# Two transformer blocks on one core: first tiles reordered behind nine warming products, bias sign on ScalarE, gate logs in steps, modulation sums three stages later, squares in one tile

## The chip, the cores and the metric

The kernel runs on one core of one Trainium2 chip. The metric is the device time of one execution in microseconds (us). Engines: PE is TensorE (PEld its weight loads), DVE is VectorE, ACT is ScalarE, POOL is GpSimd, SP issues most DMAs. Each engine works through its own instructions in program order and waits where an operand is not ready.

## The reference, cut to what matters

```python
h = concat(meta_tokens, x)                       # 16 + 512 rows of 1024
u = rms_norm(h, norm_mix); proj = u @ w_in       # q, k, v, forget logits, conv, gates
o_a = windowed attention with sinks (bias table) # 8 heads, blocks of 128
log_f = log_sigmoid(fl + fox_forget_bias)        # 8 heads x 528
o_f = attention with cumsum(log_f); o_c = gated linear recurrence
h = h + (sum of gated branches) @ w_out
h = h + (silu(u2 @ gate) * (u2 @ up)) @ w_ffn_out
x = rms_norm(h, norm_final)                      # end of block one
mod = c @ w_ada + b_ada                          # 6 x 1024, needed by block two only
z = rmsnorm(x) * (1 + scale1) + shift1           # block two: mLSTM, differential
...                                              # attention, 32 experts, top 2
```

All of it is fp32.

## The kernel before, in words

Every dense product is made from three fp32r products: operands are split into a rounded high part (ACT copies) and a remainder (DVE subtracts), and high x high, high x low and low x high are summed in one PSUM bank. A *unit* is 128 output columns: 24 products of 512 columns for a depth of 1024. `pairA` runs two units interleaved over the depth, `unitA` one. Activations are stored with features on the partitions and 528 token columns.

**Weights.** `Stream` loads tiles of 1 MB in a fixed order (`order`) through SP into three slots; `split` makes the two parts of one unit (ACT copy L492, DVE subtract L493) into three pairs of part buffers; `ahead` splits whatever finds a free pair, `fill` issues a load for every free slot. SP issues in order, and a load waits at the head of the queue until the slot's last reader is done. The modulation tiles (`ada`, 24 chunks) stand in the same order; chunk n is summed on DVE (`ada_chunk`, two instructions of 1024 elements, L561) in `after()` behind the plan entry that `ada_at` names: the 4 `wo` entries take chunks 0 to 3, the first FFN-in entries chunks 4, 5, 6 and so on.

**Interleaving by hand.** A unit calls `tick()` after its depth steps 1, 3 and 5 and at its end. `later` holds generators that each advance one step per tick, `bg` a queue of attention pipes. So a generator's `yield` says after how many products its next instructions stand in each engine's order.

**The head.** `st.first` loads the first weight tile in two halves and splits them; `v_prep` makes the high part of input tile k (L753) and its square (L755) on ACT; `v_fin` the low part (L758) and the running sum of squares (L761) on DVE. Behind `pairA` stand `sum_rows` (column sums by products with a column of ones, L698, over the two tiles `acc` and `sqs[7]`), the row scale by `rsqrt` on 5 columns, one unit, `spread` (L692), the copies to `rb` on ACT (L774, L775) and `qa_out` on DVE (L779). `u_tiles` then makes the eight normed tiles (ut L789, uh L790 on ACT, ul L793) one per tick. The bias table `nbias` (1 MB) is loaded by SP (L799) and its sign turned on POOL (L800). The units for ka and va follow; `to_natural` copies va on ACT (L814) and transposes it on PE (L818) one tick later; then the units on the normed tiles begin.

**The forget gate.** After the unit `fl`, `log_sigmoid` (Abs, Exp, Ln on ACT; L717 to L719), a subtract, a memset and a scan run on DVE (L720, L917, L918) without a tick between; the result goes to DRAM and comes back broadcast (`load_cum`, POOL queue). The attention pipe `swa` shares ACT and DVE with it: scores minus bias L849, exponent L854, scale L860, transposes on PE L870.

**The first FFN units.** f = 0, 1, 2 run on un-normed input; their outputs are scaled afterwards in `normed` (L1204 to L1208, then the split L686, L687). `f_tiles` makes the normed input for f = 3 on: nt on DVE (L1193), fh on ACT (L1194), fl on POOL (L1197), one tile per tick.

**The end of block one.** `ff_last` runs the last FFN-out units in two token halves; squares on ACT (L1273, L1276) are added on POOL (L1277) into a first tile, and tile 7 keeps its own, so that `sum_rows` reads two tiles. `z_half` then makes the row scales (L1375 to L679), spreads them on PE (L692) and makes the z tiles (L1386, L1387, L1389). `Z1` and `Z2` say how many steps of it are taken at each product group of the next stage. The shared constants' slice `LATE` holds the vector c until the last modulation sum, and is loaded with constants afterwards.

Of the kernel before, what the change touches and what calls it, by code (L numbers as in the profile page):

```python
# [20 lines left out]
D = 1024  # L21
# [22 lines left out]
Z2 = ((1, 1, 1, 1, 1, 0, 0, 0), (0, 0, 1, 0, 0, 2, 2, 2))  # L44
# [314 lines left out]
def tile_kernel(ctx: ExitStack, tc: tile.TileContext, ws, ada, c_d, hT_d, cst_d, seq_d, bd_d, wr_d, pos_d, out):  # L359
# [54 lines left out]
    class Stream:  # L414
# [32 lines left out]
        def first(self):  # L447

            t = self.slots.popleft()
            self.raw[self.order[0]] = t  # L450
            self.lp = 1
            hs = [(j, slice(512 * i, 512 * i + 512)) for i in range(2) for j in range(2)]
            v = t.rearrange("p (j c) -> p j c", j=2)
            d = ws[0].rearrange("p (j c) -> p j c", j=2)
            for _, c in hs[::2]:
                nc.sync.dma_start(v[:, :, c], d[:, :, c])
                yield
            parts = []
            for j in range(2):
                self.done[j] = self.used[j] = self.parts.popleft()  # L460
                parts.append(self.done[j])
            self.sp = 2
            for n, (j, c) in enumerate(hs):
                if n == 2:
                    yield
                h, l = parts[j]
                S.copy(h[:, c], v[:, j, c])
                V.tensor_sub(l[:, c], v[:, j, c], h[:, c].bitcast(FT))
            self.free(self.order[0])
# [66 lines left out]
    ada_at = {n_wo + n: n for n in range(n_ada)}  # L536
# [179 lines left out]
    def log_sigmoid(out_t, x, tmp):  # L716
        S.activation(tmp, x, AF.Abs)  # L717
        S.activation(tmp, tmp, AF.Exp, scale=-1.0)
        S.activation(tmp, tmp, AF.Ln, bias=1.0)  # L719
        V.scalar_tensor_tensor(out_t, x, 0.0, tmp, op0=OP.min, op1=OP.subtract)  # L720

# [14 lines left out]

    halves = st.first()
    for k in range(0, 8, 2):
        nc.sync.dma_start(hT[k // 4][:, k % 4:k % 4 + 2], hT_d[:, k:k + 2])
        if k < 6:  # L740
            next(halves)
# [4 lines left out]
    acc = SM([128, T], name="acc")  # L746
    sqs = {}

    def v_prep(k):
        if k == 3:  # L750
            for _ in halves:
                pass
        S.mul(X(vh, k), X(hT, k), C("nm", k, k + 1))  # L753
        sqs[k] = acc if k == 0 else SM([128, T], name="sq")
        S.activation(sqs[k], X(hT, k), AF.Square)  # L755

    def v_fin(k):
        V.scalar_tensor_tensor(X(vl, k), X(hT, k), C("nm", k, k + 1), X(vh, k).bitcast(FT), op0=OP.mult,  # L758
                               op1=OP.subtract)
        if 0 < k < 7:  # L760
            V.tensor_add(acc, acc, sqs[k])  # L761

    set_ring([0, 1, 2, 3])
    first = pairA(v_h, v_l, v_prep, v_fin, XS)
    sum_rows(bank[4], 0, [acc, sqs[7]], 4, NM)
    sum_rows(bank[4], 4, [acc, sqs[7]], 1, 0)
    r5 = [ST([128, 16], name=f"r5{i}") for i in range(4)]
    V.tensor_scalar(r5[0][:, :5], bank[4][:, :5], 1.0 / D, EPS, op0=OP.mult, op1=OP.add)
    rsqrt(r5[1][:, :5], r5[0][:, :5], (r5[2][:, :5], r5[3][:, :5]))
    first += unitA(v_h, v_l, one_bank)  # L770
    spread(r5[1], bank[5])
    PE.matmul(bank[6][:, :NM], lhsT=r5[1][:, 4:5].to_broadcast([128, 128]), rhs=ident[:, :NM], start=True, stop=True)
    rb = SM([128, T], name="rb")
    S.copy(rb[:, NM:], bank[5])  # L774
    S.copy(rb[:, :NM], bank[6][:, :NM])  # L775
# [5 lines left out]
    for t in range(3):  # L781
        qa_out(t, first[t])
    ut = {}
# [12 lines left out]
    ug = later.add(u_tiles())  # L796
    qa_out(3, unitA(v_h, v_l, one_bank)[0])
    nbias = B([128, 8, 256], name="nbias")
    nc.sync.dma_start(nbias, seq_d)  # L799
    G.tensor_scalar(nbias, nbias, -1.0, None, op0=OP.mult)  # L800
# [29 lines left out]
    later.finish(ug)  # L830
# [79 lines left out]
    p = uT()  # L910
    lf = SM([8, T], name="lf")
    l2 = SM([8, T], name="l2")
    cum = SM([8, T], name="cum")
    for h in range(2):
        V.tensor_scalar(cum[:, HALF[h]], p[h][:8], C("fbias")[:8], None, op0=OP.add)
    log_sigmoid(lf, cum, l2)
    V.memset(l2, 1.0)  # L917
    V.tensor_tensor_scan(cum, l2, lf, 0.0, op0=OP.mult, op1=OP.add)  # L918
    cum_d = dpool.tile([8, T], FT, name="cum_d")
    G.dma_start(cum_d, cum)  # L920
# [8 lines left out]
    load_cum(0)  # L929
# [281 lines left out]
    def ff_in(gi):  # L1211
        a0, b0 = FGROUPS[gi]
        ah, al = [], []
        for f in range(a0, b0):
# [4 lines left out]
            if f < 3:  # L1219
# [17 lines left out]
                continue  # L1237
            w = SM([128, 512], name="fw")
# [18 lines left out]
    def ff_last(gi, steps):  # L1257
# [5 lines left out]
        def part(t, cs):  # L1263
            wh, wl = us[t][1:]
            p = DB()
            mm3([(p[:, cs], cs)], lambda i: wh[:, i], lambda i: wl[:, i], ah, al, nk, mid=False)
            h = X(hx, t)[:, cs]
            V.tensor_add(h, h, p[:, cs])
            for parts, scale in ((sums, 1.0), (sums_n, C("nfin", t, t + 1))):
                if t in (0, 7):  # L1270
                    if t == 0 or cs is TOK[0]:
                        parts.append(SM([128, 512], name="sq"))
                    S.activation(parts[-1][:, cs], h, AF.Square, scale=scale)  # L1273
                else:
                    sq = SM([128, 512], name="sq")
                    S.activation(sq[:, cs], h, AF.Square, scale=scale)  # L1276
                    G.tensor_add(parts[0][:, cs], parts[0][:, cs], sq[:, cs])  # L1277
# [20 lines left out]
    G.dma_start(cst[:, LATE], cst_d[:, LATE])  # L1298
# [1053 lines left out]
```

## Time and profile before

| what | before |
|---|---|
| median of 3 runs (lowest, highest) | 1619.85 us (1619.43, 1620.01) |
| the profiled execution, its own time | 1618.47 us |
| its span from first to last instruction | 1616.7 us |
| PE busy in the span | 1537.2 us (95%) |
| DVE, ACT, POOL busy | 923.3, 657.0, 201.2 us |
| mean granted TensorE clock | 0.987 of full |
| DMA | 258.28 MB, mean 160 GB/s |

The span is cut into windows; a window tells how long each engine was busy in it, how many instructions that were, and the clock granted to PE. The list of waits says whose result an engine stood for. The timeline gives start, duration and idle time before each instruction. In the last fifth of the span the DMA engines are busy nine tenths or more of the time; before it they are not.

### The profile page before, as it was taken

The page shows a single profiled execution, that of the slowest core. Times are in us where ns is not written, and L with a number is a line of the kernel's source. Part 1 is how long each engine was busy: PE and PEld are TensorE (multiplying, and loading weights), DVE is VectorE, ACT ScalarE, POOL GpSimd, SP SyncE. Part 2 cuts the span into 40 slices and gives each one's busy share as a digit, 9 for nine tenths or more (in the row PEclk, how much of TensorE's full clock was granted, in tenths as well). Part 3 has the DMA queues.
Part 4 walks back from the last instruction along what each step waited for, and adds up shares of the span by engine and source line. Part 5 has one row for each costly group of instructions (what it writes and reads, how often), then busy time and mean ns, then how long its engine had stood idle before and what let it go on. Part 6 is the DMA issues. An engine that isn't in the chain of part 4 may idle for free. (4 is left out here: it accounts for less than half of the span.)

```text
span 1616.7 us, 22593 instructions
## 1 busy us (share of the span) xinstructions
PE 1537.2 (95%) x8524; PEld 1153.4 (71%) x8524; DVE 923.3 (57%) x2020; ACT 657.0 (41%) x1208; POOL 201.2 (12%) x255
## 2 busy tenths in 40 slices
PE   7899999999999899999999999999999999998883
PEld 6788777788888778888889887778888874433321
DVE  5655455455757676664444755873466445565443
ACT  4445443326534332222233545653233215665442
POOL 0100111020030200000002142200013102111101
PEclk9999999999999999999999999999999999999997
DMA  5221221222235255445222241222223866999992
GB/s 187 92 79 67 92 80 53 79 91 79 103 137 215 104 209 208 181 186 193 105 83 100 79 143 54 78 79 85 95 82 134 312 234 258 388 404 392 395 390 65
DMA packets 49327, 258.28 MB, mean 160 GB/s; under 512 B 7316, under 2 KB 15636, under 8 KB 21184
## 3 DMA queue, kind: packets, MB, share of 16 engines
q1 hardware_dynamic: 41680, 237.17, 38.6%
q0 software_dynamic: 7248, 19.65, 4.2%
q8 instruction: 67, 1.10, 0.3%
q14 instruction: 44, 0.36, 0.1%
q10 hardware_dynamic: 288, 0.01, 0.0%
HBM read 250.48 MB, written 14.71 MB: 164 GB/s over the span
## 5 line engine op out<-in xcount | busy, mean ns | idle before, releaser
L493 DVE TENSOR_TENSOR wp<-wr,wp 128x1024 fp32r<-128x1024 f32 (+1 forms) x198 | 246.1, 1246 | 198.5 <-ACT wp L492 197.8
L492 ACT CAST wp<-wr 128x1024 fp32r<-128x1024 f32 (+1 forms) x198 | 204.2, 1035 | 111.3 <-PE bank L601 82.2
L599 PE MATMUL bank<-uh,wp 128*128 128x512 f32 (+1 forms) x464 | 150.7, 361 | 5.5 <-DVE ka L806 4.5
L601 PE MATMUL bank<-ul,wp 128*128 128x512 f32 (+1 forms) x464 | 144.4, 348 | 0.0
L603 PE MATMUL bank<-uh,wp 128*128 128x512 f32 (+1 forms) x464 | 144.1, 347 | 0.0
L599 PE MATMUL bank<-fh,wp 128*128 128x512 f32 x304 | 119.3, 392 | 6.6 <-ACT wp L492 6.6
L603 PE MATMUL bank<-fh,wp 128*128 128x512 f32 x304 | 119.2, 392 | 0.6 <-DVE wp L493 0.5
L601 PE MATMUL bank<-fl,wp 128*128 128x512 f32 x304 | 119.1, 392 | 0.4 <-POOL fl L1197 0.4
L599 PE MATMUL bank<-z,wp 128*128 128x512 f32 x264 | 108.4, 411 | 0.0
L603 PE MATMUL bank<-z,wp 128*128 128x512 f32 x264 | 103.3, 391 | 0.0
L601 PE MATMUL bank<-z,wp 128*128 128x512 f32 x264 | 102.9, 390 | 0.0
L599 PEld LDWEIGHTS bank<-uh,wp 128*128 128x128 f32 x464 | 81.0, 190 | 24.1 <-issue 6.8
L603 PEld LDWEIGHTS bank<-uh,wp 128*128 128x128 f32 x464 | 81.1, 190 | 11.2
L601 PEld LDWEIGHTS bank<-ul,wp 128*128 128x128 f32 x464 | 81.0, 190 | 9.8
L2197 ACT COPY wd<-wb 128x512 f32 x108 | 60.7, 616 | 55.9 <-DMA wb<-in_ws_dram 21.1
L2204 PE MATMUL bank<-wd,xT 128*32 128x512 f32 x512 | 78.5, 603 | 0.9 <-DVE wd L2197 0.6
L599 PE MATMUL bank<-ah,wp 128*128 128x512 f32 (+1 forms) x218 | 76.1, 349 | 0.0
L601 PE MATMUL bank<-al,wp 128*128 128x512 f32 (+1 forms) x218 | 75.9, 348 | 0.0
L603 PE MATMUL bank<-ah,wp 128*128 128x512 f32 (+1 forms) x218 | 75.9, 348 | 0.0
L599 PEld LDWEIGHTS bank<-fh,wp 128*128 128x128 f32 x304 | 57.6, 189 | 19.2 <-ACT wp L492 7.4
L603 PEld LDWEIGHTS bank<-fh,wp 128*128 128x128 f32 x304 | 57.4, 189 | 13.6 <-DVE wp L493 1.7
L601 PEld LDWEIGHTS bank<-fl,wp 128*128 128x128 f32 x304 | 57.5, 189 | 12.8 <-POOL fl L1197 0.8
(627 smaller groups left out, 3186.5 us busy)
## 6 DMA issues: line engine op xcount, KB each, us to landing
wr<-in_ws_dram SPq DMA_DIRECT2D x115, 1024.0 KB, 4.8
wb<-in_ws_dram SPq DMA_DIRECT2D x54, 1024.0 KB, 20.3
wr<-in_ada_dram SPq DMA_DIRECT2D x24, 1024.0 KB, 5.2
wq<-in_ws_dram SPq DMA_DIRECT2D x21, 1024.0 KB, 24.0
wr<-in_ws_dram SPq DMA_DIRECT2D x4, 768.0 KB, 4.2
ncb<-cum_d POOLq DMA_DIRECT2D x8, 264.0 KB, 3.7
wr<-in_ws_dram SPq DMA_DIRECT2D x4, 512.0 KB, 5.3
h_d<-row SPq DMA_DIRECT2D x8, 256.0 KB, 4.1
```

The lines of the kernel that those rows point to most:

```text
L492: S.copy(h[:, :fl], t)
L493: eng.tensor_sub(l[:, :fl], t, h[:, :fl].bitcast(FT))
L599: PE.matmul(ps, lhsT=wh(k), rhs=rh(k, sl), start=first and k == 0, stop=False)
L601: PE.matmul(ps, lhsT=wh(k), rhs=rl(k, sl), start=False, stop=False)
L603: PE.matmul(ps, lhsT=wl(k), rhs=rh(k, sl), start=False, stop=last and k == nk - 1)
L2197: (V.tensor_copy if j < 2 else S.copy)(t[:, j], w[:, bass.ds(regs[q][j], 512)])
L2204: PE.matmul(ps[c], lhsT=x(c), rhs=w(j), start=first, stop=last)
```

## The change

Nine products of 256 columns (identity times a zeroed tile, fp32) are issued before anything else on PE. The first half of the first weight tile is loaded as two transfers of 256 columns, ahead of input tiles 2 and 3. The high and low parts of input tiles 0 and 1 come first, then the weight splits, then tiles 2 and 3; squares come after the last input tile and are all summed into `hsq[0]` on DVE. Row sums, row scale, spread, rb and the first three `qa_out` become a generator, `norm_1`, stepped inside the next two units; `sum_rows` reads one tile instead of two. The bias load is issued before those units, and its sign is turned by two ACT multiplications of 1024 columns in `norm_1`. The gate's logarithm becomes a generator with Abs and Exp, Ln, subtract, scan one or two ticks apart, and its memset goes to POOL. Modulation chunks 4 to 23 move three plan entries later, and the reload of `LATE` with them to f = 19. In `ff_last` tile 7's squares are added on POOL as well, `sum_rows` reads one tile, and the second half's sums are one product group later.

```diff
-Z2 = ((1, 1, 1, 1, 1, 0, 0, 0), (0, 0, 1, 0, 0, 2, 2, 2))
+Z2 = ((1, 1, 1, 1, 1, 0, 0, 0), (0, 0, 0, 1, 0, 2, 2, 2))
...
-            for _, c in hs[::2]:
-                nc.sync.dma_start(v[:, :, c], d[:, :, c])
+            for cs in ((slice(0, 256), slice(256, 512)), (slice(512, 1024),)):
+                for c in cs:
+                    nc.sync.dma_start(v[:, :, c], d[:, :, c])
                 yield
...
-    ada_at = {n_wo + n: n for n in range(n_ada)}
+    ada_at = {n_wo + n + (3 if n > 3 else 0): n for n in range(n_ada)}
...
+            PE.matmul(bank[7][:, :256], lhsT=ident, rhs=mbig[:, :256], start=True, stop=True)
+    warm_up(9)
...
+    def v_mul(k):
+        S.mul(X(vh, k), X(hT, k), C("nm", k, k + 1))
+        V.scalar_tensor_tensor(X(vl, k), X(hT, k), C("nm", k, k + 1), X(vh, k).bitcast(FT), op0=OP.mult,
+                               op1=OP.subtract)
+    def h_square(k):
+        hsq[k] = SM([128, T], name="sq")
+        S.activation(hsq[k], X(hT, k), AF.Square)
+        if k:
+            V.tensor_add(hsq[0], hsq[0], hsq[k])
     def v_prep(k):
-        if k == 3:
+        if k == 2:
+            v_mul(2)
+            v_mul(3)
             for _ in halves:
                 pass
...
+        elif k > 3:
+            v_mul(k)
     def v_fin(k):
...
+        if k == 6:
+            for n in (1, 2):
+                h_square(n)
+    for k in range(2):
+        v_mul(k)
+    h_square(0)
+    next(halves)
     first = pairA(v_h, v_l, v_prep, v_fin, XS)
...
+    for k in range(3, 8):
+        h_square(k)
+    def norm_1():
+        yield
+        yield
+        sum_rows(bank[4], 0, hsq[:1], 4, NM)
+        sum_rows(bank[4], 4, hsq[:1], 1, 0)
+        V.tensor_scalar(r5[0][:, :5], bank[4][:, :5], 1.0 / D, EPS, op0=OP.mult, op1=OP.add)
+        rsqrt(r5[1][:, :5], r5[0][:, :5], (r5[2][:, :5], r5[3][:, :5]))
+        for t in range(4):
+            yield
+            if t % 2 == 0:
+                S.mul(nbias[:, 2 * t:2 * t + 4], nbias[:, 2 * t:2 * t + 4], -1.0)
+        spread(r5[1], bank[5])
...
+        S.copy(rb[:, NM:], bank[5])
+        S.copy(rb[:, :NM], bank[6][:, :NM])
+        for t in range(2):
+            qa_out(t, first[t])
+        yield
+        qa_out(2, first[2])
+        ug.append(later.add(u_tiles()))
...
     nc.sync.dma_start(nbias, seq_d)
-    G.tensor_scalar(nbias, nbias, -1.0, None, op0=OP.mult)
+    later.add(norm_1())
+    first += unitA(v_h, v_l, one_bank)
+    qa_out(3, unitA(v_h, v_l, one_bank)[0])
...
+    def forget_sums(p):
...
+        S.activation(l2, cum, AF.Abs)
+        S.activation(l2, l2, AF.Exp, scale=-1.0)
+        yield
+        S.activation(l2, l2, AF.Ln, bias=1.0)
+        yield
+        yield
+        V.scalar_tensor_tensor(lf, cum, 0.0, l2, op0=OP.min, op1=OP.subtract)
+        G.memset(l2, 1.0)
+        yield
+        V.tensor_tensor_scan(cum, l2, lf, 0.0, op0=OP.mult, op1=OP.add)
+        G.dma_start(cum_d, cum)
+        load_cum(0)
+    later.add(forget_sums(uT()))
...
+            if f == 19:
+                G.dma_start(cst[:, LATE], cst_d[:, LATE])
...
-                if t in (0, 7):
-                    if t == 0 or cs is TOK[0]:
-                        parts.append(SM([128, 512], name="sq"))
-                    S.activation(parts[-1][:, cs], h, AF.Square, scale=scale)
+                if t == 0:
+                    parts.append(SM([128, 512], name="sq"))
+                    S.activation(parts[0][:, cs], h, AF.Square, scale=scale)
                 else:
...
     ff_out(0)
-    G.dma_start(cst[:, LATE], cst_d[:, LATE])
```

## Rows read from the trace of the kernel before

**Rows 1.** Windows: length; busy us (count) of PE, PEld, DVE, ACT, POOL; clock; DMA

```profile
8.80:15.00 6.20, 6.12 (x14) 4.45 (x15) 5.04 (x9) 6.20 (x12) 0.00 (x0) 1.00 1.04 420
...
23.18:25.33 2.15, 2.15 (x22) 2.15 (x20) 0.00 (x0) 1.28 (x2) 0.00 (x0) 1.00 0.00 0
25.33:29.00 3.67, 3.67 (x11) 2.90 (x11) 3.12 (x14) 0.00 (x0) 0.00 (x0) 0.54 0.02 4
...
51.10:55.62 4.52, 0.00 (x1) 0.03 (x1) 4.52 (x9) 2.33 (x4) 1.30 (x1) 1.00 0.00 0
55.62:60.00 4.38, 4.38 (x16) 3.20 (x17) 4.03 (x8) 2.01 (x4) 0.00 (x0) 0.61 0.37 97
...
138.20:140.34 2.14, 0.40 (x4) 0.18 (x2) 2.07 (x9) 0.02 (x1) 0.53 (x1) 1.00 0.05 8
140.34:145.90 5.56, 5.56 (x33) 4.54 (x33) 2.89 (x10) 3.02 (x10) 2.05 (x4) 0.69 0.44 118
...
519.60:530.40 10.80, 10.80 (x49) 8.97 (x48) 6.16 (x11) 2.76 (x4) 0.00 (x0) 1.00 0.52 200
...
554.96:560.49 5.53, 0.15 (x1) 0.00 (x0) 3.76 (x8) 2.19 (x3) 1.49 (x1) 0.77 0.53 190
560.49:564.84 4.35, 4.31 (x10) 2.97 (x10) 3.19 (x4) 2.36 (x4) 1.75 (x2) 0.51 0.00 0
564.84:577.40 12.56, 10.43 (x44) 7.66 (x43) 10.25 (x12) 4.08 (x6) 3.49 (x3) 1.00 0.46 168
...
902.52:906.25 3.73, 3.73 (x12) 2.94 (x12) 3.43 (x10) 1.02 (x2) 0.00 (x0) 0.54 0.53 138
```

**Rows 2.** Waits of PE: product <- releaser: us in total, times, longest

```profile
PE bank L631 <- ACT vh L753: 8.8, 1, 8.8
...
PE bank L599 <- ACT wp L492: 6.6, 2, 5.4
PE bank L599 <- DVE ka L806: 4.5, 1, 4.5
```

**Rows 3.** Timeline of the head, 0 to 62 us: start, duration, instruction, idle before

```profile
7.00 1.14 ACT L467 CAST wp<-wr 128x512 fp32r<-128x512 f32 x2 [4.49 <-DMA wr<-in_ws_dram]
...
33.62 0.59 ACT L774 COPY rb<-bank 128x512 f32<-128x512 f32 x1 [9.16 <-PE bank L692]
...
47.01 5.39 POOL L800 TENSOR_SCALAR nbias<-nbias 128x2048 f32<-128x2048 f32 x1 [45.52 <-DMA nbias<-in_seq_dram]
47.04 4.20 DVE L793 TENSOR_TENSOR ul<-ut,uh 128x528 fp32r<-128x528 f32 x1
...
57.87 1.05 PE L818 MATMUL bank<-ident,vt 128*128 128x128 f32 x4
```

**Rows 4.** Groups by form, 0 to 62 us: busy us, mean ns | idle before

```profile
L758 DVE SCALAR_TENSOR_TENSOR vl<-hTb,cst,vh 128x528 fp32r<-128x528 f32 x4 | 3.0, 760 | 0.0
...
L753 ACT ACTIVATE vh<-hTb,cst 128x528 fp32r<-128x528 f32 x4 | 2.9, 729 | 0.0
...
L755 ACT ACTIVATE sq<-hTb 128x528 f32<-128x528 f32 x4 | 2.5, 636 | 0.0
```

**Rows 5.** Timeline of the first FFN units: POOL, DVE and ACT

```profile
540.97 1.29 POOL L1197 TENSOR_TENSOR fl<-nt,fh 128x512 fp32r<-128x512 f32 x1 [61.95 <-ACT fh L1194]
548.52 7.93 POOL L1197 TENSOR_TENSOR fl<-nt,fh 128x512 fp32r<-128x512 f32 x4 [6.26 <-ACT fh L1194]
...
550.76 2.31 DVE L561 CUSTOM_DVE_ANT_0 wr<-wr,cst 128x1024 f32<-128x1024 f32 x1
...
559.41 1.03 ACT L492 CAST wp<-wr 128x1024 fp32r<-128x1024 f32 x1
```

**Rows 6.** Timeline behind the forget gate: PE

```profile
140.34 0.73 PE L870 MATMUL bank<-ident,sws 128*128 128x128 f32 x4 [1.75 <-DVE swm L849]
```

**Rows 7.** Timeline of the second half's row scale: DVE and PE

```profile
907.83 0.16 DVE L679 SCALAR_TENSOR_TENSOR m<-m,m 128x4 f32<-128x4 f32 x1
...
908.33 0.61 PE L692 MATMUL bank<-ident,m 128*128 128x128 f32 x4
```

## Prediction before the run

> **What bounds the kernel now.** I read the engine shares first: PE is busy 1537 of 1616.7 us, so time is lost only where PE stands or runs at half clock. The list of waits shows how little of this one releaser holds [rows 2], so next come windows around each stall [rows 1]: in each, length against PE's busy time and its count, and the granted clock. Full pace is 48 products in 10.80 us, 0.225 us each in the window 519.60 to 530.40 [rows 1]. The timelines then say what ended each stall [rows 3, 5, 6, 7]. The edits touch four stretches: the head to about 60 us, the forget gate at 138 to 146, the first FFN units at 555 to 577, and the row scales near 881 and 903. In each PE's own order waits for ACT, DVE or POOL; the DMA-filled last fifth hangs on PE's progress, so that what is won earlier should come out at the end one for one.
>
> **Head.** First product: PE waits until 8.8 [rows 2], because ACT first waits for the weights (7.00), splits two parts (1.14) and only then makes input tile 0 (0.73) [rows 3, 4]. The new order makes tiles 0 and 1 while the weights travel, so the first product needs one part copy after 7.00: 7.6 at best. It stands behind nine warming products, a form that no row has. The nearest is the spread, two fp32 products of 128 columns in 0.61 with their drain [rows 7]; 256 columns are then 0.36 to 0.6 at full clock and double at half, nine of them 3 to 11 us. I take about 6.5, as they begin while the clock is still low, so that they end near 8.2 and the first product gains 0.6; bounds: a gain of 1.2, a loss of 2. The two 256-column pieces carry the same bytes; at worst they land a little later.
>
> Pace: 14 products fill 8.80 to 15.00 [rows 1], 0.44 us each, the pace of 1.2 GHz, although the window's clock column says 1.00; at 0.225 they would take 3.0 us less. If PE has worked without pause before, I take all of 3.0; lower bound 0. The supply must then hold: eight depth steps cost PE 10.8 us, ACT without squares 8 x 0.73 plus four part copies of 0.57, 8.1 us, DVE 8 x 0.76 plus four subtracts of about a copy's length, 8.4 us [rows 3, 4]. With the squares in between (0.64 each) ACT would need 13.2 and bind: that is what moving them pays.
>
> Row sums: 20 instructions in 2.15 us [rows 1] become 10, a gain of 1.1. They now stand half a unit further on, where PE waits for the last of seven adds. ACT ends the squares about 19, DVE the adds about 21.5, PE arrives at 21.7: cost 0, up to 1.5. The half-clock stretch behind them (3.67 us at 0.54) loses 1.7; with half the tiny products between full ones I take that as gone (bounds 0 and 1.7). So PE is through the va unit at 51.1 - 0.6 - 3.0 - 1.1 - 1.7 = 44.7.
>
> Bias sign: POOL's 5.39 us stretch one DVE subtract to 4.20 instead of 0.7 [rows 3], and PE stands 4.52 us, then runs at 0.61 for 4.38 us, 1.7 lost [rows 1]. On ACT it is two instructions of 1024 columns, about 1.03 each by the copy of that size [rows 5], in a stretch where ACT is idle 9.16 us before rb [rows 3]; cost 0 while the bias has landed. It does so early: its load now stands on SP behind three weight loads, the last of which waits only for the first tile's splits. Were it late, rb and every later weight copy would stand behind it on ACT (rival C).
>
> What is late next: the spread stands half a unit later in PE's order, so rb comes near 30.5, not 34.2. From there DVE needs four qa, eight tiles of two instructions and ka, 21 instructions of 0.65 to 0.76 [rows 4], and two weight subtracts of some 1.1: 16 us, 17 with its waits for ACT; the last cast of u, and behind it on ACT the va copies, end near 47.7. PE wants the va transposes at 46.1 and gets them at 47.7, against 57.87 [rows 3]. Gain 10.2, and 0.3 of the half clock behind it: **10.5**, bounds 7 and 12.6 (all named losses).
>
> **Gate.** PE stands 2.1 us for softmax scaling on DVE [rows 6], then 5.56 us pass at 0.69 clock [rows 1], about 1.7 lost. DVE was held by the gate's subtract, memset and scan, which ran as one block behind ACT's table load. In steps, the weight subtract and the softmax go first; memset leaves DVE; the number of table loads stays, as Ln still stands between exponents. I take **2.8** of 3.8, bounds 0 and 3.8. The sums return some 6 us later, a whole unit, and are used three units on; the three tiles of the gate are held longer out of a pool of twelve, which could hold up a softmax tile instead.
>
> **FFN.** Lost here: 5.53 us standing; 4.35 us for nine products, 2.3 too many; 12.56 us for 44, 2.6 too many [rows 1]: 10.4. The chain is DVE: tile 4, then the two sums of chunk 5 (2.31 each) [rows 5], `normed`, then ACT's weight copy at 559.41, which ends PE's wait. Moving chunk 5 takes 4.6 us out ahead of `normed` of f = 1, chunk 6 some 3.5 ahead of f = 2. PE was ready at 554.96; the copy at 554.9 at best leaves 1 us of standing.
>
> But POOL is making fl tiles just there, four in 7.93 us where one alone takes 1.29 [rows 5], so instructions of `normed` now meet what the sums met. With 1 to 1.5 us added, PE starts f = 3 at about 557.2 and then waits some 1 to 2 us for fl tiles 5 to 7, still one after another on POOL. I take **6.0**, bounds 2 and 10.4.
>
> The Trainium skill, SBUF — State Buffer (SBUF: two separate sides), calls the port pair of these two engines an exclusive lock for a whole instruction. By it the subtract begun at 47.04 would end after POOL's 52.40; the trace ends it at 51.24, so it agrees in kind, not in length. By the rule four instructions of `normed` could each stand a whole fl tile, and this part would give about 2 (rival B).
>
> The moved chunks land in FFN units where DVE is busy about 60% (6.16 of 10.80, one chunk included [rows 1]); their 2.4 us are hidden, and cost that much each if not. On SP each chunk load moves three entries on, and the weight loads it preceded go earlier; the constants' reload on POOL's queue comes three FFN pairs, some 33 us, ahead of its readers.
>
> **Squares.** Each half's sums lose 8 of 16 tiny products, 0.85 us at 0.107 each [rows 1]. Tile 7 now passes through two POOL adds of about 0.65 each (half of 1.29, an estimate), hidden in the first half behind the unit that follows and one group later in the second. In the second half the saving ends at DVE: its row scale is done at 907.99 and the spread starts at 908.33 [rows 7], so PE wins 0.3 however fast it comes, and then stands about 2 us, which behind the gate was followed by half clock. The half clock at 902.52 to 906.25 (0.54) cost nothing for this reason. I take **0.5**, bounds +1.5 and -1.5.
>
> **Sum.** 10.5 + 2.8 + 6.0 + 0.5 = 19.8. The profiled execution took 1618.47 us (span 1616.7), so 1598.7; the median stands 1.4 higher: **1600.0**, range of this case alone 1595 to 1605.
>
> **Rivals.** A, the forecast, 0.62. B, the port takes the FFN gain back: four in a row of `normed` wait for POOL and only 2 us stay; for it the 7.93 us [rows 5], against it that three of seven steps of `normed` are waits of DVE anyway: 1604, chance 0.17. W, the warming does not lift the clock before the first product, or takes until 11: 3 us of the head stay lost, 1603, chance 0.07. E, every named loss goes (12.6 + 3.8 + 10.4 + 1.5): 1591.5, chance 0.06; against it that u, fl and the row scale are each late next. C, the bias lands late: if its load stood on SP as long as before, it would land at 47.0 [rows 3]; ACT would copy rb near 50.8, behind two sign turns and a weight copy, 16.6 us later than before, and the va transposes would come at 68.0, 10.1 later. With 9.3 from the rest that is 1620.7, no change; only the order of loads speaks against it: 0.05. D, **slower**: the clock is not granted through the head, because sums, spread and waits now lie between its products. It holds 33.8 us of full-pace products; all of them at half cost 33.8, the head ends 23.3 later instead of 10.5 earlier, and with 9.3 from the rest the time is 1634. It decides from some 20 us at half clock on. For it stands that the clock fell at 25.33 with PE busy throughout [rows 1]; against it that every such window of the trace is followed by one at full clock: 0.03.
>
> **How the numbers follow.** The predicted time is A's. The range of 1593 to 1609 holds A, B and W and leaves out E, C and D, 0.14. A measurement of this kernel tells 0.2%, 3 us, from no change. Faster is A, B, W and E, 0.92; within 0.2% is C, 0.05; slower is D, 0.03.
>
> **What would show it.** Right: first product near 8.2 at 0.225 us from the start; no POOL instruction at the bias, DVE's ul all near 0.7; first unit on u about 44 to 46 and va's transposes near 48 behind ACT; no L870 wait at the gate; f = 3 starting 2 us after PE is ready, waiting for fl, not 5.4 for a weight copy; the spread of the second half released by DVE. Wrong: products at 0.43 us after the warming, an ACT wait for the bias, PE waiting for the summed squares, new half-clock windows, or stalls at f = 16 to 18.

## The result and the profile after

The changed kernel takes 1602.15 us, the median of four executions (1601.27 to 1603.20), against 1619.64 for the kernel before in the same rounds (1616.96 to 1620.01): a ratio of 0.9896, 95% interval 0.9879 to 0.9913, or 17.5 us less. The forecast of 1600.0 was 2.2 us too low, inside its range. One execution of those timed for this document, of the run with squares in two tiles, took 2162.27 us at a mean granted clock of 0.65 and stands in no median.

The profiled execution took 1603.20 us. Its busy times, from the page:

```profile
PE 1533.4 (96%) x8516; PEld 1151.2 (72%) x8516; DVE 920.1 (57%) x2020; ACT 660.0 (41%) x1210; POOL 198.9 (12%) x259
```

To see where the time went, I set the same instruction of both timelines side by side and let the start after fall short of the start before. What the gain grows by between two landmarks was won between them.

| landmark (start, us) | before | after | won so far | won in the part | forecast |
|---|---|---|---|---|---|
| transposes of va | 57.87 | 48.79 | 9.1 | | |
| transposes ahead of the gate | 132.15 | 124.06 | 8.1 | head 8.1 | 10.5 |
| column sums ahead of the FFN | 530.47 | 518.91 | 11.6 | gate 3.5 | 2.8 |
| column sums, first half of block one's end | 880.97 | 863.78 | 17.2 | FFN 5.6 | 6.0 |
| spread behind the second half | 922.94 | 905.39 | 17.6 | squares 0.4 | 0.5 |

The parts make 17.6, the medians 17.5. (The two profiled spans differ by 15.3 only: the profiled execution after is the slowest of its four, and lower clock in two stretches that the change does not touch, near 1015 and 1300 us, takes 2 us back in it.) So by the medians what was won came out at the end one for one, as the forecast took it. The stretch filled by DMA is shorter than the last fifth, though: in the kernel before, the DMA engines are busy nine tenths or more from about 1360 to 1560 us, an eighth of the span, and for a short time at 1260.

Windows of the changed kernel over the stretches of [rows 1] (length; busy us and count of PE, PEld, DVE, ACT, POOL; granted clock; DMA share, GB/s):

```profile
8.30:19.80 11.50, 11.50 (x48) 9.03 (x49) 10.89 (x16) 10.89 (x18) 0.00 (x0) 1.00 1.02 415
...
22.61:23.70 1.09, 1.09 (x12) 1.09 (x10) 1.09 (x2) 0.58 (x1) 0.00 (x0) 1.00 0.05 15
46.49:48.79 2.30, 0.00 (x0) 0.00 (x0) 2.22 (x5) 1.59 (x4) 0.00 (x0) 1.00 0.81 321
48.79:53.86 5.07, 5.07 (x19) 3.78 (x19) 3.69 (x12) 2.18 (x7) 0.00 (x0) 0.66 0.36 129
124.00:131.57 7.57, 7.57 (x63) 6.45 (x62) 4.86 (x13) 7.44 (x15) 0.53 (x1) 1.00 0.00 0
543.60:545.64 2.04, 0.00 (x1) 0.01 (x1) 1.10 (x3) 1.56 (x2) 0.00 (x0) 1.00 0.00 0
545.64:554.10 8.46, 6.48 (x25) 4.39 (x26) 6.06 (x7) 3.45 (x5) 5.22 (x3) 1.00 0.11 18
888.90:890.68 1.78, 0.00 (x0) 0.00 (x1) 1.45 (x9) 0.00 (x0) 0.00 (x0) 1.00 0.70 295
```

The first pair now runs 48 products in 11.50 us, nearly the full pace of 10.80 [rows 1], with ACT and DVE busy 10.89 each: they just keep up. The row sums take 1.09 and no half clock follows. The gate's stretch has no standing and no low clock. Ahead of f = 3 PE stands 2.04 us, not 5.38, and stays at full clock. What is left is the stall of 2.30 at the transposes of va, with a clock of 0.66 behind it, and 1.78 ahead of the second half's spread. The list of PE's waits says for whom:

```profile
PE bank L847 <- ACT vt L843: 2.3, 1, 2.3
...
PE bank L600 <- ACT wp L493: 2.0, 1, 2.0
...
PE bank L693 <- DVE m L680: 1.8, 1, 1.8
...
PE bank L602 <- POOL fl L1235: 1.5, 2, 1.2
```

(Lines have moved: L843 and L847 were L814 and L818, L493 was L492, L600 to L604 were L599 to L603, L693 was L692, L1231 and L1235 were L1193 and L1197.) The timeline of the head after, to be held against [rows 3]:

```profile
1.72 6.23 PE L735 MATMUL bank<-mbig,ident 128*128 128x256 f32 x18 [1.72 <-DVE mbig L404]
8.30 0.50 PE L632 MATMUL bank<-vh,wp 128*128 128x512 f32 x1 [0.34 <-ACT wp L468]
...
4.55 1.28 ACT L750 ACT_TABLE_LOAD   x1 [4.55 <-DMA hTa<-in_hT_dram]
...
23.12 1.06 ACT L796 ACTIVATE nbias<-nbias 128x1024 f32<-128x1024 f32 x1 [1.83 <-DMA nbias<-in_seq_dram]
...
30.39 0.59 ACT L799 COPY rb<-bank 128x512 f32<-128x512 f32 x1 [1.89 <-PE bank L693]
...
47.83 0.63 ACT L819 CAST uh<-ut 128x528 fp32r<-128x528 f32 x1 [0.66 <-DVE ut L818]
48.37 0.65 ACT L843 COPY vt<-bank 128x264 f32<-128x264 f32 x2
...
48.79 0.83 PE L847 MATMUL bank<-ident,vt 128*128 128x128 f32 x4 [2.30 <-ACT vt L843]
```

The nine warming products end at 7.95 and the first real one starts at 8.30; the bias costs ACT a wait of 1.83 us, but long before rb, whose copy runs from 30.39 to 30.98; the last cast of u (uh) and the va copies behind it release PE at 48.79.

### The profile page after: what moved, and what is told of

Its sections match the earlier page's. It is cut to its first block, busy times and chain, and to the rows that moved or that the text cites. A ratio compares the mean times of both kernels' runs of the same rounds, so it can differ in the third digit from the quotient of the medians.

```text
span 1601.4 us, 22598 instructions
## 1 busy us (share of the span) xinstructions
PE 1533.4 (96%) x8516; PEld 1151.2 (72%) x8516; DVE 920.1 (57%) x2020; ACT 660.0 (41%) x1210; POOL 198.9 (12%) x259
## 5 line engine op out<-in xcount | busy, mean ns | idle before, releaser
L493 ACT CAST wp<-wr 128x1024 fp32r<-128x1024 f32 (+1 forms) x198 | 204.2, 1035 | 110.5 <-PE bank L602 84.5
L600 PE MATMUL bank<-uh,wp 128*128 128x512 f32 (+1 forms) x464 | 150.4, 360 | 1.0 <-DVE gt L1064 0.7
L604 PE MATMUL bank<-uh,wp 128*128 128x512 f32 (+1 forms) x464 | 143.8, 347 | 0.0
L600 PE MATMUL bank<-fh,wp 128*128 128x512 f32 x304 | 118.4, 390 | 2.0 <-ACT wp L493 2.0
L604 PE MATMUL bank<-fh,wp 128*128 128x512 f32 x304 | 118.4, 389 | 0.5 <-DVE wp L494 0.5
L600 PE MATMUL bank<-z,wp 128*128 128x512 f32 x264 | 109.1, 413 | 0.0
L604 PE MATMUL bank<-z,wp 128*128 128x512 f32 x264 | 103.7, 393 | 0.0
L600 PEld LDWEIGHTS bank<-uh,wp 128*128 128x128 f32 x464 | 80.8, 189 | 19.5 <-issue 6.6
L604 PEld LDWEIGHTS bank<-uh,wp 128*128 128x128 f32 x464 | 80.9, 189 | 11.3
L600 PE MATMUL bank<-ah,wp 128*128 128x512 f32 (+1 forms) x218 | 76.1, 349 | 0.0
L604 PE MATMUL bank<-ah,wp 128*128 128x512 f32 (+1 forms) x218 | 75.9, 348 | 0.0
L600 PEld LDWEIGHTS bank<-fh,wp 128*128 128x128 f32 x304 | 57.1, 188 | 14.3 <-ACT wp L493 2.5
L604 PEld LDWEIGHTS bank<-fh,wp 128*128 128x128 f32 x304 | 57.1, 188 | 12.8 <-DVE wp L494 1.0
```

The lines of the kernel that those rows point to most:

```text
L493: S.copy(h[:, :fl], t)
L600: PE.matmul(ps, lhsT=wh(k), rhs=rh(k, sl), start=first and k == 0, stop=False)
L604: PE.matmul(ps, lhsT=wl(k), rhs=rh(k, sl), start=False, stop=last and k == nk - 1)
```

## The experiments

Ten runs: nine edits of the changed kernel, and the changed kernel once more; all compute the whole reference. The new order of the first tiles, the smaller first loads and the row sums over one tile had no run of their own. To take one execution's clock out of a comparison, shifts are read between two landmarks of the timelines, as above, and the median stands beside them. One execution still differs from the next: with the same code up to there, the first product starts at 8.30 to 8.66 us and the landmark ahead of the gate stands at 122.70 to 125.38, mostly by the half clock that the last section shows.

### Without the warming products

```diff
-    warm_up(9)
+    warm_up(0)
```

> The nine warming products are left out, nothing else. Theory (the clock, not the supply of tiles, set the pace of the first products): the first product still starts near 8.3, but about 14 products take 0.44 us instead of 0.23, so that the first pair of units ends near 22.8 instead of 19.8 and everything behind it comes 3 us later: about 1605 us. Rival (ACT and DVE supply the tiles no faster than this anyhow, and the warming only hides that): the pair ends within 0.7 us of 19.8, and the time stays within 1 us of the changed kernel's 1602.

Measured: 1603.32 us (1601.41 to 1607.18). The start of PE's timeline:

```profile
8.48 0.80 PE L632 MATMUL bank<-vh,wp 128*128 128x512 f32 x1 [8.48 <-ACT wp L468]
...
12.45 0.39 PE L632 MATMUL bank<-vh,wp 128*128 128x512 f32 x1
```

Nine products fill 8.48 to 12.45, at 0.43 us from one start to the next, and from 12.45 they follow at 0.23. The unit behind the pair starts at 21.49 instead of 19.80, 1.7 later. 0.18 of that is the later first product (8.48 against 8.30), which also varies where the code is the same; the pair itself takes 13.01 instead of 11.50, so the warming is worth 1.5 us. At the transposes of va the shift is 1.68 (50.47 against 48.79); ahead of the gate it is 0.12 (124.18 against 124.06), because this execution had no half clock behind the transposes and the changed kernel's had. Against two executions that had none either (122.70 and 122.84) it is 1.5 and 1.3 there. The theory's mechanism holds, its 3 us do not: in this order of tiles PE stands at the low pace for 9 products, in the kernel before for 14 [rows 1]. What makes the difference of five was not tried. The median is 1.2 higher, within the spread.

### The bias sign on POOL, but early

```diff
     nc.sync.dma_start(nbias, seq_d)
+    G.tensor_scalar(nbias, nbias, -1.0, None, op0=OP.mult)
...
-            if t % 2 == 0:
-                S.mul(nbias[:, 2 * t:2 * t + 4], nbias[:, 2 * t:2 * t + 4], -1.0)
```

> The bias is loaded as early as in the changed kernel, but its sign is turned by POOL in one instruction, as before, instead of by two ACT multiplications. Theory (POOL's 5.4 us stretch whatever DVE does beside them): the POOL instruction runs from about 22 to 28 now, DVE's weight subtracts and the row scale beside it are stretched as the subtract of 4.20 us was, the spread (29.30 in the changed kernel) starts 2 to 4 us later, and the time is about 1605. Rival (only the place of the instruction mattered, and the early load alone moves it away from the path): the spread starts within 0.5 us of 29.3, and the time is that of the changed kernel, 1602, or up to 0.5 less since ACT is spared two instructions of 1.05.

Measured: 1605.23 us (1604.97 to 1605.91), 3.1 above the changed kernel. From the timelines of POOL, DVE and PE:

```profile
23.50 6.19 POOL L825 TENSOR_SCALAR nbias<-nbias 128x2048 f32<-128x2048 f32 x1 [22.01 <-DMA nbias<-in_seq_dram]
...
22.10 2.35 DVE L494 TENSOR_TENSOR wp<-wr,wp 128x1024 fp32r<-128x1024 f32 x2
...
24.56 5.17 DVE L674 TENSOR_SCALAR r<-r 128x5 int32<-128x5 int32 x1
...
31.79 1.44 PE L693 MATMUL bank<-ident,r 128*128 128x128 f32 x6 [2.08 <-DVE r L680]
```

The spread starts at 31.79, 2.5 later than 29.30 (0.24 of it was there at the row sums already), and PE stands 2.08 for it. So it was right to take the instruction off POOL: with the early load alone, about 3 us of the gain would be missing, by the median and at the transposes of va (52.09 against 48.79). What stood was not the weight subtracts, as the theory had it, but one step of the row scale on five columns: it takes 0.17 elsewhere and 5.17 here, and ends at 29.73, as POOL does (23.50 + 6.19 = 29.69). POOL's own instruction takes 6.19 against 5.39 [rows 3]; the 0.80 more may be the weight subtracts of DVE, which ran until 24.45, but no run tried that. The Trainium skill, SBUF — State Buffer (SBUF: two separate sides), has the one that starts first keep the shared ports for its whole instruction; this run agrees to 0.04 us, while the subtract of [rows 3] ended 1.16 us ahead of POOL.

### The gate in one block

```diff
         S.activation(l2, l2, AF.Exp, scale=-1.0)
-        yield
         S.activation(l2, l2, AF.Ln, bias=1.0)
-        yield
-        yield
...
-        G.memset(l2, 1.0)
-        yield
+        V.memset(l2, 1.0)
         V.tensor_tensor_scan(cum, l2, lf, 0.0, op0=OP.mult, op1=OP.add)
```

> The forget gate's logarithm, subtract, memset and scan stand in one block again, memset on DVE; all else as changed. Theory (DVE's block held the weight subtract and the softmax scaling, and the half clock followed from PE's standing): the PE wait for the scaled scores of about 1.75 us and the stretch at 0.69 clock behind it come back, 3.5 us between the gate and the transposes of the branch output: about 1605.6. Rival (the wait is gone because the head has shifted the weight loads and the clock windows, not because of the steps): no wait of over 0.5 us there, and the time within 0.7 us of 1602.

Measured: 1606.22 us (1604.65 to 1609.18), 4.1 above. DVE's and PE's timelines, and a window behind them (columns as above):

```profile
128.22 0.70 DVE L957 SCALAR_TENSOR_TENSOR lf<-cum,l 8x528 f32<-8x528 f32 x1 [3.34 <-ACT l L956]
...
129.62 1.25 DVE L959 TENSOR_TENSOR_SCAN cum<-l,lf 8x528 f32<-8x528 f32 x1
130.79 1.19 DVE L494 TENSOR_TENSOR wp<-wr,wp 128x1024 fp32r<-128x1024 f32 x1
...
133.57 0.92 PE L899 MATMUL bank<-ident,sws 128*128 128x128 f32 x4 [1.75 <-DVE swm L878]
```

```profile
133.57:137.90 4.33, 4.33 (x20) 3.26 (x21) 2.45 (x8) 2.46 (x8) 1.61 (x3) 0.61 0.39 125
```

DVE idles 3.34 us for ACT's Ln at the head of the block (subtract, memset, scan), while the weight subtract and the softmax scaling stand behind it in its order. The wait of 1.75 is back to the digit [rows 6], and so is the half clock. Over the gate alone the timelines drift apart by 3.6 us (1.32 at the transposes ahead of it, 4.88 behind), as the theory said. The edit put back the order and the memset on DVE together; what the memset alone costs was not tried.

### The modulation sums at their old place

```diff
-    ada_at = {n_wo + n + (3 if n > 3 else 0): n for n in range(n_ada)}
+    ada_at = {n_wo + n: n for n in range(n_ada)}
```

> Chunks 4 to 23 of the modulation sums go back to the plan entries of before (the reload of the constants stays where the change put it). Theory (DVE is the chain: chunk 5 and 6 stood ahead of the first outputs' scaling): PE's wait of about 5.4 us for the weight copy comes back ahead of f = 3, with the half clock behind it, the sums at the end of the FFN's first half come 5.6 us later, about 1607.8. Rival (POOL's fl tiles beside DVE's scaling set the end, and the sums only fill DVE's idle time): the wait grows by 2 us or less, about 1604.

Measured: 1607.97 us (1607.04 to 1608.99). Timelines of DVE and PE at f = 3:

```profile
537.98 2.32 DVE L562 CUSTOM_DVE_ANT_0 wr<-wr,cst 128x1024 f32<-128x1024 f32 x1
...
540.23 2.30 DVE L562 CUSTOM_DVE_ANT_0 wr<-wr,cst 128x1024 f32<-128x1024 f32 x1
...
547.70 0.80 PE L600 MATMUL bank<-fh,wp 128*128 128x512 f32 x1 [5.38 <-ACT wp L493]
548.29 0.63 PE L602 MATMUL bank<-fl,wp 128*128 128x512 f32 x1
```

The two sums stand in front of the scaling of the second output (f = 1), PE waits 5.38 us for the weight copy, and the products behind it run at 0.43. From 1.28 us ahead of the changed kernel's profile at the sums ahead of the FFN (517.63 against 518.91), this one falls to 4.37 behind it at the sums of the first half (868.15 against 863.78): 5.6, all that the FFN part won. The rival, that POOL's fl tiles bind, falls: the wait grew by 3.3, not by 2 or less.

### The fl tiles on DVE

```diff
-                G.tensor_sub(X(fl, k - 1), ws_.pop(k - 1), X(fh, k - 1).bitcast(FT))
+                V.tensor_sub(X(fl, k - 1), ws_.pop(k - 1), X(fh, k - 1).bitcast(FT))
```

> The remainders of the FFN's normed input tiles (fl) are made on DVE (about 0.70 us each, as the same subtract on the first block's tiles) instead of POOL. Theory (POOL's subtracts stretch DVE's: an nt of 1.78 and one product of 1.67 where the same forms take 0.75 and 0.69 alone): both fall to about 0.7, which gives 2.0 of the 4 x 0.70 that DVE takes on ahead of f = 3, so that f = 3 starts 0.5 to 1 us later than now, the later waits for fl (0.21 and 1.25) go, and the sum is within 0.7 us of the changed kernel. Rival (the long ones have another cause): they stay, f = 3 starts 2.8 us later, 1.5 of it is won back behind it, and the time is 1.3 us or more above the changed kernel's 1602.

Measured: 1603.87 us (1601.59 to 1606.26). First the changed kernel's own rows ahead of f = 3, then those of this run:

```profile
529.95 1.36 DVE L1244 SCALAR_TENSOR_TENSOR fw<-fw 128x512 f32<-128x512 f32 x1 [0.70 <-ACT fw L1243]
...
537.54 1.78 DVE L1231 SCALAR_TENSOR_TENSOR nt<-hxb,cst,rb 128x512 f32<-128x512 f32 x1
540.62 1.67 DVE L1244 SCALAR_TENSOR_TENSOR fw<-fw 128x512 f32<-128x512 f32 x1 [0.70 <-ACT fw L1243]
...
537.03 6.41 POOL L1235 TENSOR_TENSOR fl<-nt,fh 128x512 fp32r<-128x512 f32 x4 [6.26 <-ACT fh L1232]
...
545.64 0.50 PE L600 MATMUL bank<-fh,wp 128*128 128x512 f32 x1 [2.04 <-ACT wp L493]
```

```profile
530.14 0.69 DVE L1244 SCALAR_TENSOR_TENSOR fw<-fw 128x512 f32<-128x512 f32 x1 [0.70 <-ACT fw L1243]
...
538.87 0.74 DVE L1231 SCALAR_TENSOR_TENSOR nt<-hxb,cst,rb 128x512 f32<-128x512 f32 x1
540.91 0.69 DVE L1244 SCALAR_TENSOR_TENSOR fw<-fw 128x512 f32<-128x512 f32 x1 [0.70 <-ACT fw L1243]
...
544.77 0.50 PE L600 MATMUL bank<-fh,wp 128*128 128x512 f32 x1 [0.98 <-ACT wp L493]
...
553.29 0.51 PE L602 MATMUL bank<-fl,wp 128*128 128x512 f32 x1 [1.89 <-DVE fl L1235]
```

The long instructions were POOL's doing: 1.78 and 1.67 become 0.74 and 0.69. That much of the theory holds. But f = 3 starts earlier, not later (PE's wait falls from 2.04 to 0.98). The theory missed two things in its count: a third long instruction goes as well (1.36 at 529.95 becomes 0.69), and only three of the subtracts, about 0.6 each from start to start, stand ahead of f = 3's weights on DVE, not four of 0.70. And the later waits for fl do not go, the last grows from 1.25 to 1.89, as DVE now makes them behind its other work. In this execution seven products at 0.43 followed that wait. Where the tiles are made is a matter of a microsecond either way; the medians (1603.87 and 1602.15) cannot tell the two apart.

### Squares in two tiles again

```diff
-Z2 = ((1, 1, 1, 1, 1, 0, 0, 0), (0, 0, 0, 1, 0, 2, 2, 2))
+Z2 = ((1, 1, 1, 1, 1, 0, 0, 0), (0, 0, 1, 0, 0, 2, 2, 2))
...
-                if t == 0:
-                    parts.append(SM([128, 512], name="sq"))
-                    S.activation(parts[0][:, cs], h, AF.Square, scale=scale)
+                if t in (0, 7):
+                    if t == 0 or cs is TOK[0]:
+                        parts.append(SM([128, 512], name="sq"))
+                    S.activation(parts[-1][:, cs], h, AF.Square, scale=scale)
```

> The squares of tile 7 keep a tile of their own again and the row sums read two tiles, with the second half's sums at the product group of before; all else as changed. Theory (the saving of tiny products is real, the second half's end is DVE's row scale): 0.4 to 0.5 us come back between the first half's sums and the second half's spread, about 1602.6. Rival (the sums one group earlier let DVE's row scale end earlier, which is worth more than eight tiny products): the second spread comes 0.5 us or more sooner, 1601.5 or less.

Measured: 1601.87 us, the median of three (1601.04 to 1602.91), ratio 0.9898 (0.9878 to 0.9918). PE's timeline of the second half in this run, then a window behind the sums, then the changed kernel's sums and spread:

```profile
882.23 1.84 PE L699 MATMUL bank<-ones,sq 128*128 128x1 f32 x16
889.75 0.61 PE L693 MATMUL bank<-ident,m 128*128 128x128 f32 x4
```

```profile
883.93:887.66 3.73, 3.73 (x12) 2.92 (x12) 3.43 (x10) 1.02 (x2) 0.00 (x0) 0.54 0.49 160
```

```profile
884.80 0.95 PE L699 MATMUL bank<-ones,sq 128*128 128x1 f32 x8
...
890.68 0.71 PE L693 MATMUL bank<-ident,m 128*128 128x128 f32 x4 [1.78 <-DVE m L680]
```

In the changed kernel the sums are eight products, and the spread follows a wait of 1.78 for DVE. Here there are sixteen, nine products at 0.43 behind them (883.93 to 887.66, 1.7 us lost, as at 902.52 to 906.25 before [rows 1]), and no wait. So in the second half the change saves both the eight products and the half clock, and PE stands for DVE's row scale instead, which in the old form ends at 889.42, only 0.3 ahead of the spread. From the sums of the first half (862.36 against 863.78, 1.42 earlier than the changed kernel's profile) to the second spread (889.75 against 890.68, 0.93 earlier) the old form loses 0.5 us, all of it in the first half. That is the theory's size, but the medians do not show it (1601.87 here, 1602.15 for the change); it rests on the landmarks of one execution each.

### The transposes of va later

```diff
         for h in range(2):
             S.copy(t[:, HALF[h]], p[h])
         yield
+        if r is not None:
+            yield
+            yield
         q = DB()
```

> The transposes of va stand two ticks, about twelve products or 2.8 us, later in PE's order. Theory (PE's wait of 2.30 us for ACT's copies is all that stands there, and the half clock that followed it in some executions needs the wait): no wait over 0.3 us and no products of 0.43 us before 56; against the changed kernel's profile 2.3 to 4.2 us, against its median 2.3 to 3.5: about 1599. Rival (the attention pipe behind needs the transposed va, or the first unit on the normed tiles needs them from ACT and DVE as late): the wait returns at another product, and 0.5 us or less is won.

Measured: 1599.33 us (1598.43 to 1600.34), ratio 0.9881 (0.9865 to 0.9898). PE's timeline:

```profile
49.92 0.60 PE L850 MATMUL bank<-ident,vt 128*128 128x128 f32 x4
...
50.38 0.48 PE L600 MATMUL bank<-uh,wp 128*128 128x512 f32 x1
```

No wait, and no product at the low pace behind. From 54.55 in the changed kernel's profile, this one is 4.17 us ahead, 2.30 of it the wait. Against an execution that had the same wait and no half clock behind it (squares in two tiles), it is 2.7 ahead at the gate (119.98 against 122.70). The stall named as "late next" in the forecast was thus one reordering away from being gone.

### ACT's table earlier, seven warming products

```diff
-    warm_up(9)
+    tb = TN([128, 16], name="tb")
+    S.copy(tb[:, :1], ones)
+    warm_up(7)
```

> A one-column ACT copy ahead of the warming products makes ACT load its table in its idle first 4.5 us instead of behind the first input tile's arrival, and seven warming products are issued instead of nine. Theory (the load of 1.28 us is on the path: it delays ACT's first tiles and the weight copy that releases PE): the first product starts near 7.1 instead of 8.3 at 0.23 us from the start, the first pair ends near 18.7, and 1.0 to 1.2 us stay to the end: about 1601. Rival (the weights land at about 7.6, and ACT only waits there instead): the first product within 0.3 us of 8.3 and no change; or the clock is not up after seven, and up to nine products at 0.43 take 1.7 back.

Measured: 1602.52 us (1599.67 to 1603.91). ACT's and PE's timelines:

```profile
1.23 1.28 ACT L738 ACT_TABLE_LOAD   x1 [1.23 <-PEq L2378]
...
7.20 1.14 ACT L468 CAST wp<-wr 128x512 fp32r<-128x512 f32 x2 [0.51 <-DMA wr<-in_ws_dram]
...
7.87 0.50 PE L632 MATMUL bank<-vh,wp 128*128 128x512 f32 x1 [1.12 <-ACT wp L468]
```

The table load moves into idle time, but ACT then waits 0.51 for the weights, so only 0.43 of the hoped 1.0 to 1.2 is won in this execution (8.30 to 7.87): the rival with the landing weights is nearer. The products run at 0.23 from 8.94 on, so the clock is up after seven. The median is no lower than the changed kernel's.

### The two together, and the changed kernel again

> Two edits together: va's transposes two ticks later, and ACT's table loaded in its idle first stretch with seven warming products instead of nine. Theory (the first is worth 2.3 us and a half clock that comes in part of the executions, the second 0.4, since the first weights land at 7.2, and both lie on the path in series): 1598.9, 3 us or more under the changed kernel in the same rounds. Rival (the head's gain is taken back where the second half's spread or the DMA-filled last fifth sets the end): 1.5 us under the changed kernel or less.

Both edits above: 1598.21 us (1596.82 to 1600.15), ratio to the kernel before 0.9873 (0.9856 to 0.9889). The changed kernel in the same rounds:

> The changed kernel unaltered, timed on the same chip and in the same rounds as the next one, so that the two can be compared. Expected 1602, within the spread of 1601 to 1604 seen so far. In its profile the products behind the transposes of va either run at 0.43 us for some 4 us or not at all: the stall ahead of them is the same 2.3 us in each profile so far, and if the half clock is there in this one and not in others of the same code, it is a matter of the execution; if it always were there in this code, the edits of the others would have removed it.

It took 1601.98 us (1600.46 to 1605.96). So the two edits win 3.8 us over the change, and 21.3 over the kernel before (1619.49); every execution of this version was faster than every one of the changed kernel in the same rounds. In its timeline the first product starts at 7.40, and the shift against the changed kernel's profile is 0.90 there and 5.25 behind the transposes of va; at the last spread it is still 5.20 (900.19 against 905.39), so nothing up to there takes it back. Here ACT found the weights there at 6.73, where it had waited for them until 7.20 in the run before: what the earlier table load gives varies with that landing, 0.43 and 0.90 at the first product of the two executions, against the changed kernel's profile. In the repeat's profile the stall of 2.30 is followed by half clock again.

## Why the prediction was right, and where its sizes were off

**Head: 10.5 forecast, 8.1 measured.** The chain went as described: first product 8.30 (forecast 8.2), full pace from it, sums at half their length, no half clock behind them, spread not held by the squares, the va unit done at 44.94 (forecast 44.7), every ul near 0.7. The sizes that were off lie on the way from rb to the gate. rb is there at 30.98 (30.39 plus 0.59), 0.5 after the 30.5 of the forecast, whose arrival at the row sums (21.7) counted 10.8 for the first pair where it took 11.50. DVE's 17 us came out as 16.8 (30.98 to 47.79, the end of the last ut). "The last cast of u, and behind it on ACT the va copies, end near 47.7": cast and copies release PE at 48.79, 1.0 behind that ut, for which the forecast had left 0.2. So the transposes come 1.1 late. And "0.3 of the half clock behind it" was to go; instead 48.79 to 53.86 runs at 0.66, much as 55.62 to 60.00 did before at 0.61 [rows 1], and 1.0 of the gain is lost between the transposes and the gate. The forecast left a stall there, and had noted behind another stall of about 2 us that half clock followed. But this last size is in part a matter of the execution: with the same code up to the gate, two executions reach it at 122.70 and 122.84 without half clock and one at 125.38 with a long one, so that the head won anything from 6.8 to 9.5.

**The price of the warming.** The pace of 0.44 was taken to cost 3.0 us. The first pair did get shorter by nearly that (14.35 before, from 8.83 to 23.18, and 11.50 after), but without the nine products it takes 13.01: 1.5 belongs to them, and 1.3 to the rest of the change in the head, which no run takes apart. Rival W did not come, as the clock was up at the first product. That the kernel without the nine takes 1603.32, near W's 1603, is chance: W took 3 us off a forecast of 1600, and the run lost 1.2 from 1602.15.

**Gate: 2.8 forecast, 3.5 measured.** The whole loss went. It was 3.5 and not 3.8: the forecast read 2.1 us of standing from a window of 2.14 that holds 0.40 of products [rows 1]; PE stands 1.75 [rows 6], and 1.7 is the half clock. The forecast took a part of it only. The experiment puts 3.6 on the block's order.

**FFN: 6.0 forecast, 5.6 measured.** PE stands 2.04 us ahead of f = 3 (forecast 2), then 0.53 for a weight subtract and 1.46 for fl (forecast 1 to 2). Of f = 1's `normed` one instruction was stretched by POOL in full (1.67 for 0.69) and one in part (0.87 for 0.69), 1.2 in all where the forecast had 1 to 1.5; rival B, with four of them, fell.

**Squares: 0.5 forecast, 0.4 measured**, with the spread released by DVE after 1.78 of standing (forecast about 2), and no half clock behind it, which had been left open.

**Rivals C, D and E.** The bias landed by 23.12, 7 us ahead of rb; the clock held through the head, except behind the one stall. E, with every named loss gone, did not come either: PE still stands at the va transposes, at f = 3 and at the second spread.

**How near the sum was.** Against the forecast the head is 2.4 short, the FFN 0.4 and the squares 0.1, and the gate gives 0.7 more: 2.2, the miss of the total. Without the gate, which was put under its full loss, it would have been 2.9.

## What to carry to other kernels

When a stall is removed, the next one on the same chain is worth moving in the same edit: the forecast named the va copies, and two `yield`s there gave 2.7 us against an execution without half clock and 4.2 against one with it, about as much as the gate. Allow for a small DVE instruction beside a long POOL one to stand for what is left of POOL's: 0.17 became 5.17 here. It is not so for each: the step ahead of it, from a PSUM bank, took 0.15 beside the same POOL instruction (24.37), and the two multiplications from a bank in `normed` took 0.68 and 0.69 beside the fl tiles (539.24 and 542.39). And read a gain of under a microsecond from landmarks that stand close together in two timelines, with the clock behind each stall compared first; the executions of one kernel spread by 2 us or more.

## What the runs showed of the hardware that was not expected

**The same stall, with and without half clock.** Eight profiled executions have PE stand 2.29 to 2.31 us at the transposes of va. Behind it some products ran at 0.43 us in five of them, and none in three, while the instructions from the first pair to the stall were the same in all eight. In the profile after they lie between 50.49 and 53.86:

```profile
50.10 0.59 PE L600 MATMUL bank<-uh,wp 128*128 128x512 f32 x1
...
53.48 0.54 PE L604 MATMUL bank<-uh,wp 128*128 128x512 f32 x1
53.86 0.39 PE L600 MATMUL bank<-uh,wp 128*128 128x512 f32 x1
```

From the end of the stall to the twentieth product behind it, the three without take 6.65 to 6.69 us, four of the others 8.16 to 8.21 and one 9.51: 1.5 to 2.9 us from one execution to the next, as much as the executions of one kernel spread. What decides it stayed open.

**A five-column instruction of 5.17 us.** Before, POOL's long instruction had been seen to stretch a full-width subtract; that a step of 0.17 can stand as long, and so hold the ten steps of the row scale behind it, is what makes the place of such an instruction matter.

**The same table load, early or late.** In the changed kernel ACT's first table load starts at 4.55, when the first tile has landed, though it needs none of it; a one-column copy in front moved it to 1.23. Before, it stood at 1.23 as well:

```profile
1.23 1.28 ACT L467 ACT_TABLE_LOAD   x1 [1.23 <-PEq L2338]
```

There ACT's first instruction was the copy of the weights, which waits until 7.00, and the load did not wait with it. So the later load came with the change, which puts input tile 0 first on ACT; the forecast did not price it. Why the one first instruction holds the load back and the other does not, no run here shows.
